# Second MLP weights' block sums made where they are used, on VectorE; q/f/g block sums per pair by accumulating transfers

## The chip, the cores and the metric

The kernel runs on one core of a Trainium2 chip. It is one program on five engines: TensorE (PE in the profile; PEld is its loading of the stationary operand), VectorE (DVE), ScalarE (ACT), GpSimd (POOL) and SyncE (SP), which only issues transfers here. Each engine works through its own list of instructions in order and waits on semaphores. Sixteen DMA engines carry the transfers. PE writes to the eight banks of PSUM, the other data lie in SBUF, inputs and intermediate results in DRAM. The metric is the device time of one execution in microseconds (us), as the median of several.

## The reference

A decoder trunk on x of 1024 tokens by 1024 features, float32, two layers. Each layer is a token mixer and a squared-ReLU MLP, each followed by a residual sum and a layer norm.

```python
def hgrn2_mixer(h, w_in, lb, norm_g, w_out):       # layer 0
    q, fz, v, g = jnp.split(h @ w_in, 4, axis=-1)  # w_in: (1024, 4096)
    q = silu(q); f = lb + (1 - lb) * sigmoid(fz); k = 1 - f
    # 8 heads of 128; S_t = diag(f_t) S_{t-1} + k_t v_t^T, o_t = S_t^T q_t
    o = recurrence(q, k, v, f)
    o = rms_norm(o) * norm_g                       # per head
    return (o * silu(g)) @ w_out

def conformer_conv_mixer(h, ...):                  # layer 1
    a, gate = split(h @ w_pw1 + b_pw1)
    u = depthwise_conv(a * sigmoid(gate), width 31, causal) + b_dw
    return silu(layer_norm(u)) @ w_pw2 + b_pw2

for i in range(2):
    x = layer_norm(alpha * x + mixer(x))
    x = layer_norm(alpha * x + square(relu(x @ w1[i])) @ w2[i])   # w1: (1024, 4096), w2: (4096, 1024)
```

## The kernel before

Every product is made in three matmuls: each float32 operand is cut into a rounded high part and the rest (ScalarE casts, VectorE subtracts: `cut`, `split`), and high x high, high x low and low x high are added in PSUM.

The large products of layer 0 and both second MLP products also use a two by two block scheme with seven products instead of eight. Four blocks of each operand are combined into seven forms, numbered and taken in `ORDER = (1, 2, 6, 5, 7, 3, 4)`. With weight blocks w0 to w3, the forms are w0 (1), w1 (2), w0 + w2 + w3 (6), w2 + w3 (5), w0 + w2 (7), the sum of all four (3) and w3 (4). Where and by whom these sums are made is what this case is about.

The stages, in order of time:

- **Value product** (to about 100 us). x and the value weights are loaded; `add_v` makes the weights' sums, half on POOL (`pool_add`), half on VectorE; `v_products` makes the seven products, `v_out` stores the values to DRAM (`vd`).
- **Pairs and recurrence** (about 100 to 600 us). Twelve pairs in the order `PAIRS`: the q and f columns of a head, or the g columns of two heads. `pair_load` (L534) brings a pair's four blocks in two loads of 512 KB into `r0` and `r1`; `pair_forms` (L542) cuts the forms, with four adds per pair on POOL, and loads the next pair when the last form is cut. `pair_product` (L737) makes one form's 12 matmuls; after every third matmul comes a `slot`, which lets the recurrence take steps at the pace `pace[1]` and counts a tick. `recurrence` (L591) is a generator of steps for one head and half of the tokens: VectorE products, small float32 matmuls, the root mean square (`ss`, with a power on POOL, L472), the result to DRAM (`od`). `swish` and `gate_out` form o * silu(g); for the first seven heads the products of the g gate are on POOL.
- **Output projection and the first MLP product** of layer 0, with norm, whose hidden forms go to DRAM (`hf`).
- **Second MLP product of layer 0** (`down_all`, about 1000 to 1300 us): seven forms times eight column blocks `c`. A column block takes 24 matmuls, one form of the weights (`fw`, tile `dw`, raw tile `dr`, six raw tiles) and one of the hidden values (`fh`, tile `dh`). `Slots.load` loads 512 KB, casts on ScalarE and subtracts on VectorE, four blocks ahead. `spare`, called for five of eight of the made forms in this stage, cuts later weights beside it: one load of 512 KB (`next`) and two stores (`ready`).
- **Convolution mixer** (1300 to 1700 us): 19 of the 31 taps on VectorE, 12 on POOL with the products made on ScalarE. Then the **first and second MLP products of layer 1** (the second from about 1950 us, without `spare`).

The block sums of both layers' w2 are made in DRAM by `block_sums` (L367): 16 calls, one per layer and column block. Each call writes two numbers of a result to the sum's tile (L371, so that the copies start only when that result is there), copies 2 x 1 MB from DRAM to DRAM on SyncE's queue (L372, L373), and adds, later by `gap` ticks each, in three accumulating transfers issued by POOL (L374 of 1 MB, L376 of 512 KB twice). Four calls lie in the value product, ten in the recurrence after a result `o`, two in the convolution stage. `form` then picks what `plan_down` loads.

To about 600 us the orders of PE, POOL and SyncE are those of the program text; VectorE's and ScalarE's orders, and from there on all, are set by a planner at build time.

Of the kernel before, what the change touches and what calls it, by code (L numbers as in the profile page):

```python
# [15 lines left out]
P = 128  # L16
D = 1024
# [18 lines left out]
KBYTES = 220  # L36
NPOOL = 12
# [71 lines left out]
class Forms(Slots):  # L109
# [40 lines left out]
    def ahead(self, n):  # L150

        while self.todo and len(self.queue) < n:
            units = self.todo[0]
            if isinstance(units[0], tuple):
                units = self.todo[0] = [self.unit(*u) for u in units]
            if all([next(u, units) is None for u in units]):
                continue
            self.todo.pop(0)

# [77 lines left out]
def body(ctx, tc, d, out):  # L237
# [127 lines left out]
    sums = {}  # L365

    def block_sums(name, layer, c, after, gap=0):  # L367

        t = sums[name, layer, c] = dram.tile([4, P, 1024], F32, name=f"sum_{name}{layer}{c}")
        v, w = t.rearrange("a p n -> p a n"), d[name][layer, c].rearrange("a p n -> p a n")  # L370
        nc.sync.dma_start(out=t[0:4:2, 0, 0:1], in_=after)  # L371
        nc.sync.dma_start(out=v[:, 0:2], in_=w[:, 0:4:2])  # L372
        nc.sync.dma_start(out=v[:, 2:4], in_=w[:, 0:2])  # L373
        parts = [lambda: nc.gpsimd.dma_start(out=v[:, 0:2], in_=w[:, 2:4], accum_op=ALU.add)]  # L374
        for i in (2, 3):
            parts.append(lambda i=i: nc.gpsimd.dma_start(out=v[:, i], in_=v[:, i - 1], accum_op=ALU.add, max_dma_last_dim=4096))  # L376
        for i, part in enumerate(parts):
            later((i + 1) * gap, part)

    to_sum = [(*of, c) for of in (("w2", 0), ("w2", 1)) for c in range(NFC)]  # L380

    def form(name, layer, c, i):

        w, t = d[name][layer, c], sums[name, layer, c]
        return {1: w[0], 2: w[1], 6: t[2], 5: t[1], 7: t[0], 3: t[3], 4: w[3]}[i]

# [30 lines left out]
    def load_v(raw, m, i0):  # L417
        for j in range(2):
            nc.sync.dma_start(out=raw[:, j], in_=d["wv"][m, i0 + j])
# [44 lines left out]
    nc.sync.dma_start(out=par, in_=d["par"])  # L464
    make_identity(nc, ident)
# [8 lines left out]
    def pool_add(out, x, y):  # L474
        pool.tensor_tensor(out=out, in0=x, in1=y, op=ALU.add)

# [12 lines left out]
    add_v(s7, a0, a2)  # L489
# [9 lines left out]
    outs_v(5)  # L499
    v_products(5)  # L500

    for k in range(4):
        pool.tensor_tensor(out=x01[:, k], in0=x11[:, k], in1=x01[:, k], op=ALU.subtract)
        cut_x(7, x01, (k,))
# [7 lines left out]
    add_v(a1, a0, a1)  # L512
# [16 lines left out]
    r0, r1 = raws((112, 116)).views  # L529
    rs7, vs = view(120, wide_t, F32, "s7"), ring(run(122, 3, 2), rows, "v")  # L530
    fs = ring((152, 156, 128, 132), (2, HT), "fs", F32R)
    PAIRS = [("q", 0), ("q", 1), ("q", 2), ("g", 0), ("q", 3), ("q", 4), ("g", 1), ("q", 5), ("q", 6), ("g", 2), ("q", 7), ("g", 3)]

    def pair_load(p):  # L534
        kind, j = PAIRS[p]
        w = d["wqf" if kind == "q" else "wg"][j]
        nc.sync.dma_start(out=r0, in_=w[0])
        nc.sync.dma_start(out=r1, in_=w[1])

    made = []  # L540

    def pair_forms(p):  # L542
        b0, b1, b2, b3 = r0[:, :HT], r0[:, HT:], r1[:, :HT], r1[:, HT:]

        def put(raw):
            s = fs()
            cut(s[:, 0], s[:, 1], raw)
            made.append(s)

        put(b0)  # L550
        pool_add(rs7, b0, b2)
        pool_add(b2, b2, b3)
        yield
        put(b1)
        pool_add(b0, b2, b0)
        yield
        put(b0)
        pool_add(b1, b0, b1)
        yield
        put(b2)  # L560
        yield
        put(rs7)
        yield
        put(b1)
        yield
        put(b3)
        if p + 1 < len(PAIRS):
            pair_load(p + 1)
        yield

# [20 lines left out]
    def recurrence(h, half):  # L591
# [98 lines left out]
        if 2 * h + half < 10:  # L690
            block_sums(*to_sum.pop(0), o[:2, 0, :1], 24)
# [15 lines left out]
    def swish(out, t, ps=None):  # L707
        sg = p1("sq")
        if ps is None:
            nc.scalar.activation(sg, t, AF.Sigmoid)  # L710
            (vector if out is not t else pool).tensor_tensor(out=out, in0=t, in1=sg, op=ALU.mult)
# [77 lines left out]
    def gate_out(h, half):  # L789
# [3 lines left out]
        def rest():  # L793
            pool.tensor_tensor(out=u, in0=u, in1=g, op=ALU.mult)
# [67 lines left out]
    pair_load(0)  # L862
    forms = pair_forms(0)
    for _ in range(4):
        next(forms)
# [8 lines left out]
            "kt": (rows, 1), "o": (rows, 2), "on": (wide_t, 1), "u": (wide_t, 2), "mask": ((3, P), 1), "rm": ((2, P), 1), "state": ((P,), 2),  # L874
# [3 lines left out]
    rm = p1("rm")  # L878
# [4 lines left out]
    nc.gpsimd.memset(rm, 1.0)  # L883
    load_values(0)

    def all_forms():
        yield from forms
        for p in range(1, len(PAIRS)):
            yield from pair_forms(p)

    ahead_of = all_forms()
    next(ahead_of)
    for p, (kind, j) in enumerate(PAIRS):
        st = {"banks": dict(turn_of)}
        turn_of = {"z": turn_of["a"], "a": turn_of["b"], "b": turn_of["z"]}
        pace[1] = 222 / 308 if p else 0.0
        for i in ORDER:
# [4 lines left out]
            next(ahead_of, None)  # L902
# [248 lines left out]

    def plan_down(layer, fw, fh):
        fw.plan([form("w2", layer, c, i) for i in ORDER for c in range(NFC)])
# [119 lines left out]
    fw = Slots(nc, vector, slots([112, 120, 144, 152, 128, 136, 168], "dw"), raws([192, 196, 200, 204, 160, 164], "dr"), spare, 5, range(12, 56))  # L1273
# [133 lines left out]
    def normalise(half):  # L1407
# [12 lines left out]
        if half == 1:  # L1420
            for of in to_sum:
                block_sums(*of, mv[:2, 0, 4:5])
# [56 lines left out]
    for op, i in steps:  # L1479
# [19 lines left out]
        else:  # L1499
# [3 lines left out]
            if i == NFC - 2:  # L1503
                fw = Slots(nc, vector, slots([64, 72, 144, 152, 200, 208, 112], "dw"), raws([132, 136, 140, 104, 108, 176], "dr"))
# [31 lines left out]
def _layout(inputs):  # L1536
# [14 lines left out]
    r["wqf"] = c(np.stack([cols(w[:, :D], H), cols(w[:, D : 2 * D], H)], 1)).reshape(H, 2, P, 1024)  # L1551
    r["wv"] = c(wide(w[:, 2 * D : 3 * D])).reshape(2, 4, P, 1024)
    r["wg"] = c(cols(w[:, 3 * D :], H)).reshape(H // 2, 2, P, 1024)
# [47 lines left out]
```

## Time and profile before

| | |
|---|---|
| median of 3 runs | 2255.55 us (2252.13 to 2256.26) |
| the profiled execution | 2262.96 us, span 2261.2 us, mean granted clock 0.973 |
| PE busy | 2129.0 us, 94% of the span |
| VectorE, ScalarE, POOL busy | 1471.6, 1034.0, 492.6 us |
| moved by DMA | 508.64 MB, 225 GB/s on average |
| accumulating transfers (software queue) | 33.56 MB |

The page gives each engine's busy time, the span in 40 slices of 56.5 us (busy share in tenths; the granted clock of PE; what the DMA engines moved), the chain of work that ended last, and groups of instructions: line, engine, operation, output<-inputs, shape, count | busy us, mean ns of one | idle time before them and what ended it. A line can be that of a helper: L172 stands for every operation issued through the planner's wrappers. Windows are tables of such numbers for a stretch of time. A busy PE is a PE with a matmul under way; how many matmuls start per microsecond tells more.

### The profile page before, as it was taken

The numbers are of one execution on the slowest core, as the hardware profiler recorded it, in microseconds if no ns is written. First come the engines' busy times: TensorE is split into PE (matmuls) and PEld (weight loads), VectorE is DVE, ScalarE is ACT, GpSimd is POOL, SyncE is SP. The second block draws the span as 40 slices with busy tenths as digits, with TensorE's granted clock in tenths as the row PEclk, the third lists the DMA queues.
The fourth block names the chain that finished last, engine by engine and source line by source line (L and its number), as shares of the span: only waits on it lengthen the run. The fifth ranks groups of instructions, "written<-read, shape, count | busy, mean of one in ns | idle before, by whom it ended". The sixth has DMA issues, their size and how long they took to land.

```text
span 2261.2 us, 27315 instructions
## 1 busy us (share of the span) xinstructions
PE 2129.0 (94%) x10056; PEld 1758.2 (78%) x10056; DVE 1471.6 (65%) x1970; ACT 1034.0 (46%) x1607; POOL 492.6 (22%) x426
## 2 busy tenths in 40 slices
PE   7969878598999999999999999999999999999998
PEld 5747666476788888888888888888887888888887
DVE  8458667476677766665666789789935544555446
ACT  5234243243414655554444477737752543443333
POOL 2231334342110000000000179739700000000001
PEclk8979989798999999999999999999999999999999
DMA  5964868853523777689999875566377798866552
GB/s 201 245 151 131 224 178 207 210 125 103 205 72 124 271 242 278 210 293 380 325 340 339 293 273 193 181 241 235 133 242 252 262 328 309 329 217 191 194 167 103
DMA packets 170952, 508.64 MB, mean 225 GB/s; under 512 B 16192, under 2 KB 45120, under 8 KB 169792
## 3 DMA queue, kind: packets, MB, share of 16 engines
q1 hardware_dynamic: 161856, 473.32, 59.3%
q0 software_dynamic: 8960, 33.56, 8.2%
q8 instruction: 79, 1.29, 0.2%
q14 instruction: 57, 0.47, 0.1%
HBM read 377.32 MB, written 196.61 MB: 254 GB/s over the span
## 4 chain that ended last, share of the span: by engine, by line
PE 75%; DMA 9%; DVE 7%; POOL 4%; issue 2%; ACT 2%; SPq 0%; DVEq 0%; POOLq 0%; ACTq 0%
PE ps L172 75%; POOL cb L172 3%; DMA raw<-in_wqf_dram 2%; DVE qk L172 2%; DMA raw<-in_wg_dram 1%; DMA vd<-vo 1%; DMA u<-od 1%; DMA wa<-ready 1%; DMA raw<-in_w_dram 1%; DVE fs L172 1%; DVE kd L172 1%; DMA vr<-in_wv_dram 1%; DVE at L172 0%; ACT fs L389 0%; POOL raw L172 0%
## 5 line engine op out<-in xcount | busy, mean ns | idle before, releaser
L172 PE MATMUL ps<-dw,dh 128*128 128x512 f32 x2688 | 611.1, 390 | 0.0
L172 PEld LDWEIGHTS ps<-dw,dh 128*128 128x128 f32 x2688 | 504.3, 188 | 104.4 <-ACT dh L69 0.2
L172 PE MATMUL ps<-xf,fs 128*128 128x512 f32 x1008 | 287.7, 425 | 27.5 <-ACT t L752 25.7
L172 PE MATMUL ps<-x1f,fw 128*128 128x512 f32 x1344 | 308.8, 391 | 0.7 <-DVE fw L172 0.3
L172 PEld LDWEIGHTS ps<-x1f,fw 128*128 128x128 f32 x1344 | 251.3, 188 | 53.0 <-DVE fw L172 0.8
L172 PE MATMUL ps<-xa,wa 128*128 128x512 f32 x1152 | 268.8, 392 | 0.0
L172 PEld LDWEIGHTS ps<-xa,wa 128*128 128x128 f32 x1152 | 214.3, 188 | 43.4
L172 POOL TENSOR_TENSOR cb<-cb,prod 128x512 f32<-128x512 f32 x176 | 234.3, 1340 | 17.6 <-ACT prod L1369 7.1
L172 PEld LDWEIGHTS ps<-xf,fs 128*128 128x128 f32 x1008 | 188.6, 200 | 63.3 <-ACT t L752 26.7
L172 DVE TENSOR_TENSOR dh<-dh 128x1024 fp32r<-128x1024 f32 x112 | 136.4, 1223 | 119.5 <-ACT dh L69 116.2
L172 DVE SCALAR_TENSOR_TENSOR ps<-u,par,ps 128x512 f32<-128x512 f32 x288 | 198.7, 750 | 9.8 <-ACT ps L1381 8.4
L172 DVE TENSOR_TENSOR dw<-dr,dw 128x1024 fp32r<-128x1024 f32 x112 | 136.6, 1223 | 101.8 <-ACT dw L69 101.2
L472 POOL TENSOR_TENSOR mv<-mv,nhalf 128x1 f32<-128x1 f32 x32 | 46.3, 1448 | 668.8 <-DVE mv L172 668.8
L69 ACT CAST dh<-dh 128x1024 fp32r<-128x1024 f32 x112 | 117.0, 1051 | 149.7 <-DMA dh<-hf 148.0
L69 ACT CAST dw<-dr 128x1024 fp32r<-128x1024 f32 x112 | 117.4, 1053 | 135.6 <-PE ps L172 124.0
L172 PE MATMUL ps<-xc,wa 128*128 128x512 f32 x768 | 174.4, 389 | 0.0
L172 PEld LDWEIGHTS ps<-xc,wa 128*128 128x128 f32 x768 | 144.1, 188 | 29.8
L1369 ACT ACTIVATE prod<-u,par 128x512 f32<-128x512 f32 x176 | 125.3, 722 | 54.2 <-POOL cb L172 53.5
L1234 POOL COPY next<-ss 128x1 f32<-128x1 f32 x37 | 16.4, 442 | 489.8 <-DVE spare L172 236.1
L172 PE MATMUL ps<-qk 128*128 128x128 f32 (+2 forms) x640 | 60.8, 256 | 59.9 <-DVE qk L172 51.7
L172 PEld LDWEIGHTS ps<-qk 128*128 128x128 f32 (+2 forms) x640 | 54.5, 167 | 78.8 <-issue 39.5
L172 DVE TENSOR_TENSOR wa<-raw,wa 128x1024 fp32r<-128x1024 f32 x55 | 71.3, 1299 | 67.6 <-ACT wa L69 67.5
(193 smaller groups left out, 2908.1 us busy)
## 6 DMA issues: line engine op xcount, KB each, us to landing
wa<-ready SPq DMA_DIRECT2D x122, 512.0 KB, 5.0
dh<-hf SPq DMA_DIRECT2D x112, 512.0 KB, 3.6
ready<-spare SPq DMA_DIRECT2D x74, 512.0 KB, 5.3
sum_w<-in_w_dram SPq DMA_DIRECT2D x32, 1024.0 KB, 7.2
dr<-sum_w SPq DMA_DIRECT2D x64, 512.0 KB, 6.4
raw<-in_w_dram SPq DMA_DIRECT2D x51, 512.0 KB, 4.5
dr<-in_w_dram SPq DMA_DIRECT2D x48, 512.0 KB, 5.3
raw<-in_w1q_dram SPq DMA_DIRECT2D x36, 512.0 KB, 4.2
```

Of the source, the lines that this page charges most:

```text
L69: self.nc.scalar.copy(out=slot[:, 0, c], in_=raw[:, c])
L172: return op(*args, **kw)
L472: nc.gpsimd.tensor_tensor(out=dst, in0=src, in1=nhalf[:, :n], op=ALU.pow)
L1234: nc.gpsimd.tensor_copy(out=raw[:, :1], in_=now)
L1369: nc.scalar.activation(tp, u[:, k : k + HT], AF.Copy, scale=tap(j, k))
```

## The change

It has four parts.

1. `block_sums` and `form` go. A class `Blocks` takes the place of `Slots` for `fw` in both second MLP products. For each form it loads the blocks or pair sums it needs: forms 1 and 2 load two blocks, cut the first, add the second to it on VectorE and store that pair's sum to DRAM; forms 6, 5 and 3 load two and add them on VectorE; 7 and 4 load one.
2. The q, f and g weights lie together (`wp`), and `pair_sums` makes each pair's sums in DRAM, of half the size: two copies of 512 KB on SyncE, accumulating transfers on POOL of 512, 256 and 256 KB. The first three pairs' are issued during the value product, the others three pairs ahead. Each form is loaded by itself (256 KB, five raw tiles, `load_form`, `make_form`). Two sums of value weights (`vsum`) are made in the same way and take the place of two `add_v`.
3. What POOL did elementwise up to 600 us (adds of the value weights, a subtraction on x, the g gate's products) goes to VectorE or falls away with the sums. The convolution's adds stay on POOL.
4. In `recurrence`, the reciprocal is made contiguous (`rt`), the product for `kd` covers half the elements, ScalarE copies the other half, and there is one more step; the pace is 240/308 instead of 222/308.

```diff
+class Blocks(Slots):
...
+    def load(self, pieces=1):
+        (i, c), slot = self.todo.pop(0), self.slots()
+        self.queue.append(slot)
+        w, pair = self.blocks[c]
+        srcs = {1: (w[0], w[2]), 2: (w[1], w[3]), 6: (pair[0], w[3]), 5: (w[2], w[3]), 7: (pair[0],), 3: (pair[0], pair[1]), 4: (w[3],)}[i]
+        got = [self.raws() for _ in srcs]
+        for raw, src in zip(got, srcs):
+            self.nc.sync.dma_start(out=raw, in_=src)
+        if i in (1, 2):
+            self.split(slot, got[0])
+            self.vector.tensor_tensor(out=got[1], in0=got[1], in1=got[0], op=ALU.add)
+            self.nc.sync.dma_start(out=pair[i - 1], in_=got[1])
+        else:
+            if len(got) > 1:
+                self.vector.tensor_tensor(out=got[0], in0=got[0], in1=got[1], op=ALU.add)
+            self.split(slot, got[0])
...
+    def pair_sums(t, w, gap, half=False):
+        n = 1 if half else 2
...
+        nc.sync.dma_start(out=flat(t)[:, 0:2], in_=flat(w)[:, 0 : 4 : n] if n == 2 else flat(w)[:, 0:2])
+        if n == 2:
+            nc.sync.dma_start(out=flat(t)[:, 2:4], in_=flat(w)[:, 0:2])
+        parts = [lambda: nc.gpsimd.dma_start(out=flat(t)[:, 0:2], in_=flat(w)[:, 2:4], accum_op=ALU.add)]
+        for i in (2, 3) if n == 2 else (1,):
+            parts.append(lambda i=i: nc.gpsimd.dma_start(out=flat(t)[:, i], in_=flat(t)[:, i - 1], accum_op=ALU.add, max_dma_last_dim=4096))
...
-            if t == 0 and i in (5, 6, 7, 3):
-                block_sums(*to_sum.pop(0), VO[{5: 5, 6: 6, 7: 5, 3: 6}[i]][0][:2, :1], 24)
+            if t == 3 and i in (2, 5, 6):
+                p = {2: 0, 5: 1, 6: 2}[i]
+                pair_sums(psum[p], d["wp"][p], 8)
...
-        pool_add(out[:, 0], x[:, 0], y[:, 0])
-        vector.tensor_tensor(out=out[:, 1], in0=x[:, 1], in1=y[:, 1], op=ALU.add)
+        for j in range(2):
+            vector.tensor_tensor(out=out[:, j], in0=x[:, j], in1=y[:, j], op=ALU.add)
...
-    add_v(s7, a0, a2)
...
+    sum_v(s7, 0)
+    sum_v(a1, 1)
...
+    def load_form():
...
+        loaded.append(praw())
+        nc.sync.dma_start(out=loaded[-1], in_={1: w[0], 2: w[1], 6: t[2], 5: t[1], 7: t[0], 3: t[3], 4: w[3]}[i])
+
+    def make_form():
+        if loaded:
+            s, raw = fs(), loaded.pop(0)
             cut(s[:, 0], s[:, 1], raw)
             made.append(s)
+            load_form()
...
-        rt = totals[4]
-        vector.reciprocal(cutout(rm, 0, [[P + 1, 2], [2, P // 2]]), cutout(rt, 0, [[1, 2], [2, P // 2]]))
-        kd = p1("kd")
-        mul(kd.rearrange("p a (b n) -> p a b n", n=4), B.rearrange("p a (b n) -> p a b n", n=4), cutout(rm, 0, [[P, 2], [1, P], [0, 4]]))
+        rt, kd = p1("rt"), p1("kd")
+        vector.reciprocal(rt, totals[4])
+        nc.scalar.copy(out=cutout(kd, 4, other), in_=cutout(B, 4, other))
+        mul(cutout(kd, 0, mine), cutout(B, 0, mine), cutout(rt, 0, [[1, 2], [2, P // 2], [0, 4]]))
+        yield
         grow(4)
...
-            pool.tensor_tensor(out=u, in0=u, in1=g, op=ALU.mult)
+            mul(u, u, g)
...
-        pace[1] = 222 / 308 if p else 0.0
+        pace[1] = 240 / 308 if p else 0.0
...
-            next(ahead_of, None)
+            make_form()
+            if i == 6 and p + 3 < len(PAIRS):
+                pair_sums(psum[p + 3], d["wp"][p + 3], 12)
...
-    fw = Slots(nc, vector, slots([112, 120, 144, 152, 128, 136, 168], "dw"), raws([192, 196, 200, 204, 160, 164], "dr"), spare, 5, range(12, 56))
+    fw = Blocks(down_weights(0), nc, vector, slots([112, 120, 144, 152, 128, 136, 168], "dw"), raws([192, 196, 200, 204, 160, 164], "dr"), spare, 5, range(12, 56))
...
-                fw = Slots(nc, vector, slots([64, 72, 144, 152, 200, 208, 112], "dw"), raws([132, 136, 140, 104, 108, 176], "dr"))
+                fw = Blocks(down_weights(1), nc, vector, slots([64, 72, 144, 152, 200, 208, 112], "dw"), raws([132, 136, 140, 104, 108, 176], "dr"))
```

More of the change, by code (lines that the diff above doesn't have):

```diff
@@ L363, in tick, with flat @@
                 job()
[L365 to L376, printed above, removed]
-        for i, part in enumerate(parts):
[L378 to L385, printed above, removed]
+    def pair_sums(t, w, gap, half=False):
+        n = 1 if half else 2
+        def flat(x):
+            return x.rearrange("a p n -> p a n")
+        nc.sync.dma_start(out=flat(t)[:, 0:2], in_=flat(w)[:, 0 : 4 : n] if n == 2 else flat(w)[:, 0:2])
[4 more added lines that the diff above has]
+            parts.append(lambda i=i: nc.gpsimd.dma_start(out=flat(t)[:, i], in_=flat(t)[:, i - 1], accum_op=ALU.add, max_dma_last_dim=4096))
+        parts.append(lambda: summed.append(t))
+        for i, part in enumerate(parts):
+            later((min(i, len(parts) - 2) + 1) * gap, part)
+    summed = []
     def cut(hi, lo, raw):
@@ L860, in last_head @@
         into(half, H - 1, u)
-    pair_load(0)
-    forms = pair_forms(0)
+    for _ in range(5):
+        load_form()
     for _ in range(4):
-        next(forms)
+        make_form()
     v_products(3)
@@ L882, in body @@
         nc.gpsimd.memset(t, 0.0)
-    nc.gpsimd.memset(rm, 1.0)
     load_values(0)
[L886 to L892, printed above, removed]
+    make_form()
     for p, (kind, j) in enumerate(PAIRS):
@@ L1150, in up_half, with down_weights @@
             store(layer, c, i, None, src)
+    def down_weights(layer):
+        return [(d["w2"][layer, c], [dram.tile([P, 1024], F32, name=f"pair{layer}{c}{k}") for k in range(2)]) for c in range(NFC)]
     def plan_down(layer, fw, fh):
[L1153 removed]
+        fw.plan([(i, c) for i in ORDER for c in range(NFC)])
         fh.plan([hf[layer][c][i] for i in ORDER for c in range(NFC)])
```

81 lines of the change are left out of this document (32 added, 49 removed).

## Prediction

> **What bounds the kernel now.** I read the page's slices first, then the windows by stage, then the waits of TensorE and of SyncE, then the chain. From the page:
>
> ```profile
> span 2261.2 us, 27315 instructions
> PEclk8979989798999999999999999999999999999999
> DMA  5964868853523777689999875566377798866552
> PE 75%; DMA 9%; DVE 7%; POOL 4%; issue 2%; ACT 2%; SPq 0%; DVEq 0%; POOLq 0%; ACTq 0%
> ```
>
> The granted clock is below full only in the first ten slices. DMA is nearly full in slices 19 to 22, where the first layer's second MLP product runs. The windows (length; busy us and count of PE, weight loads, DVE, ACT, POOL; clock, DMA share, GB/s) say the same with numbers:
>
> ```profile
> 0.00:100.00 100.00, 83.73 (x336) 67.14 (x336) 69.27 (x81) 40.45 (x62) 25.78 (x23) 0.93 0.69 218
> 100.00:150.00 50.00, 26.29 (x102) 20.96 (x102) 24.08 (x40) 16.30 (x28) 16.07 (x17) 0.80 0.97 232
> 150.00:600.00 450.00, 370.06 (x2177) 304.76 (x2177) 301.77 (x523) 164.55 (x401) 141.21 (x109) 0.91 0.59 160
> 154.30:188.30 34.00, 33.61 (x225) 27.83 (x224) 27.07 (x52) 15.02 (x34) 4.62 (x4) 1.00 0.32 107
> 450.00:500.00 50.00, 44.62 (x288) 36.64 (x287) 39.72 (x71) 20.17 (x51) 19.83 (x16) 0.97 0.57 137
> 1000.00:1300.00 300.00, 300.00 (x1339) 248.57 (x1338) 189.17 (x212) 136.31 (x142) 18.85 (x32) 1.00 0.93 337
> 1000.00:1020.00 20.00, 20.00 (x90) 16.58 (x89) 10.50 (x11) 6.61 (x8) 1.69 (x4) 1.00 1.02 377
> 1020.00:1060.00 40.00, 40.00 (x178) 33.00 (x177) 23.84 (x26) 19.03 (x19) 1.42 (x2) 1.00 1.03 407
> 1700.00:1800.00 100.00, 96.75 (x437) 79.61 (x436) 53.95 (x67) 34.26 (x47) 8.85 (x6) 0.98 0.71 243
> 1950.00:2250.00 300.00, 300.00 (x1325) 248.50 (x1324) 168.03 (x169) 123.61 (x131) 9.59 (x7) 1.00 0.58 200
> 1960.00:1980.00 20.00, 20.00 (x90) 16.57 (x89) 12.34 (x11) 9.65 (x10) 0.00 (x0) 1.00 1.03 414
> ```
>
> So there are two kinds of stage. From 150 to 600 us (q/f/g pairs beside the recurrence) PE starts 4.84 matmuls per us, but 6.62 in an undisturbed stretch (154.3 to 188.3). Both second MLP products (1000 to 1300, 1950 to 2250) keep PE full: anything that delays them is paid whole. What delays the first stage is in PE's waits (us, times, longest; up to 150 us, then 150 to 600), SyncE's waits and three pieces of the chain:
>
> ```profile
> PE ps L172 <- DVE qk L172: 13.6, 1, 13.6
> PE ps L172 <- ACT t L752: 9.2, 1, 9.2
> ```
> ```profile
> PE ps L172 <- DVE qk L172: 42.4, 16, 6.2
> PE ps L172 <- ACT t L752: 16.4, 2, 10.2
> ```
> ```profile
> SPq L371 <- ACT o L689: 130.1, 10, 27.5
> SPq L795 <- POOL u L172: 108.2, 11, 19.9
> ```
> ```profile
> 227.53 12.13 DMA raw<-in_wqf_dram
> ...
> 317.38 12.63 DMA raw<-in_wg_dram
> ...
> 348.93 14.89 DMA raw<-in_wqf_dram
> ```
>
> A pair's two weight loads have one buffer each. They are issued behind a block sum that waits for a recurrence's output (L371), they run beside its DRAM copies, and they take 12 to 15 us each time on the chain. The pool adds, the cuts on DVE and the recurrence line up behind them; the gated output's store (L795) waits for POOL's product too.
>
> **The change part by part.** Instructions and transfers it touches, as groups and DMA rows (the POOLq rows and those with 5.4 and 7.2 us: median from issue to landing; the L87 row: shortest, median, longest issue in ns; the second fence is of 1000 to 1300 us alone):
>
> ```profile
> L172 POOL TENSOR_TENSOR t<-t,sq 128x512 f32<-128x512 f32 x12 | 18.1, 1510 | 80.4 <-ACT sq L710 80.4
> L172 POOL TENSOR_TENSOR u<-u,t 128x512 f32<-128x512 f32 x12 | 18.0, 1501 | 55.3 <-DMA u<-od 39.3 <-DVE ss L172 16.0
> L172 DVE TENSOR_TENSOR qk<-qk,f 128x512 f32<-128x512 f32 x28 | 19.2, 687 | 0.2
> L172 DVE TENSOR_TENSOR kd<-qk,rm 128x1024 f32<-128x1024 f32 x16 | 24.6, 1540 | 0.3 <-PE ps L172 0.3
> L389 ACT CAST fs<-raw 128x512 fp32r<-128x512 f32 x72 | 43.8, 620 | 149.2 <-PE ps L172 70.5 <-DMA raw<-in_wqf_dram 31.3 <-DMA raw<-in_wg_dram 26.2
> L69 ACT CAST dw<-dr 128x1024 fp32r<-128x1024 f32 x112 | 117.4, 1053 | 135.6 <-PE ps L172 124.0 <-issue 3.9 <-DMA hf<-hr 3.2
> L172 DVE TENSOR_TENSOR dw<-dr,dw 128x1024 fp32r<-128x1024 f32 x112 | 136.6, 1223 | 101.8 <-ACT dw L69 101.2
> sum_w<-in_w_dram POOLq DMA_DIRECT2D x16, 1024.0 KB, 12.4
> sum_w<-sum_w POOLq DMA_DIRECT2D x32, 512.0 KB, 7.2
> L87 SPq DMA_DIRECT2D dr<-sum_w x64: 319/320/1614, 1032.3 to 2141.5; - x64
> ```
> ```profile
> DMA packets 29050, 101.20 MB, mean 337 GB/s; under 512 B 3168, under 2 KB 4192, under 8 KB 29032
> ready<-spare SPq DMA_DIRECT2D x48, 512.0 KB, 5.4
> dr<-in_w_dram SPq DMA_DIRECT2D x15, 512.0 KB, 7.2
> ```
>
> Pairs, 150 to 600 us: ten block sums leave (2 MB of copies and 2 MB of accumulating transfers each), with the SyncE wait of 130.1 us. Twelve half-size sums come, three pairs ahead, and every form has its own 256 KB load, five buffers deep and some ten forms before use: 84 loads for 24. At the best 50 us (450 to 500: 288, or 5.76 per us) 2177 matmuls take 378 us, 72 less. Bounds: only the waits behind `t` go (-16), or all runs at 6.62 (329 us, -121). I take -72, because that window still holds waits but few of them.
>
> Its cover: DVE takes 24 products from POOL (24 x 0.69 = 17 us); the half-length kd product saves 16 x (1.54 - 0.69) = 14; the reciprocal keeps its size. DVE's 302 us become 305 of 378, 81%, and the undisturbed stretch has 80% with PE full. ACT gets 16 copies of 0.62 us (10 us) on 165 of 450, SyncE 60 more issues of 0.32 us (19 of 378): nothing. The recurrence has 18 steps for 17 and a pace 240/222 as fast: nothing. Without DVE's cover this is the second rival. POOL's power op now stands behind accumulating transfers that wait for one another (12.4 and 7.2 us at twice the size); issues lie 12 of a pair's 28 slots apart (of 378 / 12 = 31 us: 13 us). On SyncE a sum's load waits for its transfer, and the recurrence's stores and value loads queue behind it; the forms' lead of some ten covers the loads, the stores have none. Bounds for both 0 and +12 (one landing of 12.4), I take +4, nearer the end where the issues are 13 us apart.
>
> Start, 100 to 150 us: the two waits of 22.8 us hang on the first pair loads, queued behind stores and sums. Now the loads go ahead but four of seven forms come from transfer sums. Bounds -5 and -25; I take -18.
>
> Value product, to 100 us: two sums move from engines to transfers (the s7 form needs one after a 12.4 us landing), other adds from POOL to DVE, which has 69 of 100 us busy and loses a competitor. Bounds -3 and +10; I take +2, nearer the end where a load comes in time.
>
> The last two block sums (near 1660 us) leave: PE misses 3.3 us from 1700 to 1800; I take -3, bounds 0 and -5.
>
> First layer's second product, from 1000 us: per column block, seven loads of 0.524 MB become twelve and two stores: 40 loads and 16 stores more, 29.4 MB. 101.2 + 29.4 = 130.6 MB. The rate decides, since DMA is at 93% already. At 407 (loads alone) they take 321 us, +21; at 337 (as now, stores a third) 388 us, +87. I take 377, the slice with both: 346 us, +46, less 6 for the blocks fetched ahead of 1000 us: +40. DVE gets 40 adds of 1.22 us: 189 + 49 = 238 of 300, beside.
>
> Here a rule speaks against the change: the Trainium skill, DMA: Bandwidth & Descriptors, Where 436 GB/s comes from, says that for transfers between HBM and SBUF a core's HBM share of about 358 GB/s binds, not the fabric. The 407 and 414 GB/s rows contradict it for loads. By the rule this term would be 365 - 300 - 6 = 59, estimated from the page, and the time 2236.
>
> Second layer: the same 29.4 MB on 200 GB/s. Only the first two forms are tight: 16 blocks of 4 transfers, 2.1 MB in 5.4 us of PE (24 x 300/1339). At 377 that is 5.6 us, +3. Also six raw tiles serve three blocks in flight, and a tile is free again only after landing 7.2, cast 1.05, two DVE ops 2.4 and the store 5.4: 16.1 us, or 5.4 per block, with nothing to spare. Bounds 0 and 16 x 2.1 = 34 (landing and store 10 us); I take +8.
>
> Sum: -72 + 4 - 18 + 2 - 3 + 40 + 8 = -39. The profiled execution took 2262.96 us (span 2261.2), which gives 2224; the median of the runs shown is 7.4 lower, so 2217.
>
> **The rivals.**
> 1. The tile ring: SyncE is one queue, so a pair's store that waits for its add holds up the next loads, and at a full DMA landing and store take 10 us: 23.5 us per three blocks, 7.8 per block. 32 blocks x 2.4 = 77; the first layer's other three two-load forms at 337 GB/s (2.6 MB with the spare traffic, 7.6 us) add 24 x 2.2 = 53. 130 instead of 48: 2299, slower. It decides from 87 us on. For it: 93% DMA and a loop without slack; against: 407 GB/s is there when asked for.
> 2. DVE becomes the bound of the pairs: 42.4 us of PE waits are on the recurrence's qk. At 5.2 matmuls per us the stage takes 419 (-31) and the start gives 8: 2268, slower. Against it: the stretch at 6.62 with DVE at 80%.
> 3. The transfers fit: 407 GB/s (+15) and nothing in the second layer: 2184.
> 4. Mixed loads and stores can't go above today's 337 GB/s: +81 instead of +40: 2258, no change. For it: the 377 slice is 20 us short; against: no engine waited at 337, so it was a demand.
>
> The page's 2236 lies between rival 4 and the forecast, inside the forecast's own range.
>
> That it doesn't do what it says touches only the convolution, whose adds stay on POOL; nothing is priced there.
>
> **How the numbers follow.** Forecast 0.40 (own range 2195 to 2240), rival 1 0.18, rival 2 0.12, rival 3 0.20, rival 4 0.10. Forecast and 3 are faster, 0.60, and 0.04 of 4; slower are 1 and 2, 0.30; same (within 0.2%, 4.5 us, which is what a measurement here can tell) 0.06 of 4. The range 2175 to 2278 holds all but rival 1 and the tails.
>
> **What would show it.** Right: PE starts on out-projection some 85 us earlier, the waits on pair loads are gone, and the window after it at full clock; the first layer's second product takes about 340 us with DMA near 1.0 and PE waiting for ACT or DVE on dw. Wrong: PE still full there (rival 3), DMA well under 1.0 while PE waits and SyncE waits on a pair's add (rival 1), or DVE above 90% from 100 to 500 us (rival 2).

## The result, and the profile after

The changed kernel takes 2246.9 us (median of six runs, 2244.3 to 2249.6) against 2254.5 (six runs, 2251.9 to 2256.7). The ratio is 0.9967 with a 95% interval of 0.9954 to 0.998: 0.3% faster, 8 us where 39 were forecast. The profiled execution took 2245.4 us. From its page (the span, the granted clock, DMA's busy share and the chain):

```profile
span 2243.3 us, 27717 instructions
PEclk9999999999999999999999989999999999999999
DMA  9866655434358687899997955375455898999762
PE 44%; DMA 5%; POOL 3%; DVE 3%; ACT 2%; issue 1%; SPq 0%; DVEq 0%; POOLq 0%; ACTq 0%
```

No slice of the first ten falls under nine tenths of the clock any more (from 100 to 150 us it is still 0.86, for 0.80 before), and a new drop stands in slice 24 (1290 to 1346 us), in the convolution. PE's 44% of the chain can't be set against the 75% before: this chain could be followed back to 912 us only, so that its shares add up to 58% of the span, where those of the kernel before add up to 99%. The stages, from the timeline (each lasts from its first matmul to the first of the next; us; the first column is when the output projection starts, the last ones the span of the profiled execution and the median of all runs). The rows below the first two are the experiments. Each was run beside the kernel before, whose median was 2254.5 to 2260.3 us in these sessions; the ratios given further down go by the runs beside:

| kernel | pairs end | output projection and 1st product, layer 0 | 2nd product, layer 0 | convolution, and first half of layer 1's 1st product | its second half | 2nd product, layer 1 | span | median |
|---|---|---|---|---|---|---|---|---|
| before | 586.6 | 411.7 | 308.4 | 467.6 | 174.2 | 312.6 | 2261.2 | 2254.5 |
| changed | 491.1 | 411.4 | 350.5 | 495.1 | 174.1 | 321.1 | 2243.3 | 2246.9 |
| early copies | 496.4 | 410.2 | 330.6 | 462.3 | 174.1 | 320.9 | 2194.5 | 2194.9 |
| before, early copies | 585.4 | 411.0 | 312.2 | 466.8 | 174.2 | 312.2 | 2261.8 | 2262.6 |
| before, late copies | 584.2 | 411.6 | 336.4 | 508.7 | 174.2 | 312.6 | 2327.7 | 2327.5 |
| one store | 491.6 | 410.6 | 351.0 | 490.4 | 174.1 | 312.7 | 2230.4 | 2233.1 |
| no store | 492.0 | 410.6 | 367.7 | 464.1 | 174.1 | 335.0 | 2243.5 | 2245.5 |
| ten raw tiles | 488.1 | 410.5 | 353.3 | 494.9 | 174.1 | 316.5 | 2237.5 | 2240.9 |
| block sums alone | 507.7 | 411.1 | 354.3 | 494.9 | 174.1 | 320.5 | 2262.5 | 2260.7 |
| the rest alone | 619.6 | 410.6 | 308.5 | 467.2 | 174.2 | 312.7 | 2292.8 | 2294.6 |
| early copies, one store | 493.2 | 410.7 | 321.1 | 464.0 | 174.1 | 312.6 | 2175.7 | 2179.6 |
| and gates on VectorE | 491.9 | 410.8 | 319.8 | 463.1 | 174.1 | 312.7 | 2172.4 | 2174.5 |
| and copies still earlier | 492.2 | 417.6 | 336.8 | 462.6 | 174.1 | 313.3 | 2196.6 | 2198.0 |
| before again | 584.9 | 411.4 | 308.3 | 469.3 | 174.2 | 312.6 | 2260.7 | 2258.9 |

So the first stage gave 95.5 us, and three later stages took back 42.1, 27.5 and 8.4. The windows of the changed kernel that answer to those before (length; busy us and count of PE, weight loads, DVE, ACT, POOL; clock, DMA share, GB/s):

```profile
0.00:100.00 100.00, 87.55 (x360) 70.74 (x360) 58.59 (x86) 42.01 (x64) 11.86 (x19) 0.97 0.95 278
100.00:150.00 50.00, 35.32 (x177) 29.16 (x178) 28.91 (x57) 20.53 (x34) 6.59 (x8) 0.86 0.68 169
150.00:490.00 340.00, 318.51 (x2013) 265.12 (x2012) 252.89 (x511) 162.05 (x398) 40.72 (x38) 0.98 0.53 148
902.50:1253.00 350.50, 319.63 (x1377) 260.37 (x1375) 231.09 (x251) 136.73 (x143) 31.90 (x40) 0.96 0.92 353
1253.00:1748.00 495.00, 471.27 (x2145) 386.99 (x2145) 376.95 (x529) 284.86 (x446) 257.27 (x202) 0.97 0.56 200
1922.00:2243.00 321.00, 307.58 (x1346) 253.52 (x1344) 212.58 (x213) 124.01 (x133) 10.46 (x8) 0.98 0.74 270
```

From 150 to 490 us PE starts 5.92 matmuls per us (4.84 from 150 to 600 before). Both second products and the convolution have lost their full PE. The convolution stage before, as a window:

```profile
1306.70:1774.40 467.70, 463.94 (x2146) 383.81 (x2144) 362.63 (x520) 275.46 (x434) 260.92 (x203) 1.00 0.62 216
```

Not all of the loss is idle time. PE is busy for 471 us in place of 464 with the same matmuls, at a clock of 0.97 in place of 1.00, so 7 of the convolution's 27.5 us are slower matmuls. In the first layer's second product it is 320 us in place of 308 at 0.96, 11 of the 42.1. PE's waits in the first of these products, and then in the convolution stage (1250 to 1750 us; in the same stage before, only 3.2 us for `wa<-ready` and 0.3 for `cb`; the wait for `xa` ends at 1251.3 us, ahead of the stage's first matmul as the table counts it):

```profile
PE ps L201 <- ACT dw L70: 15.1, 4, 8.8
PE ps L201 <- ACT dh L70: 10.2, 1, 10.2
```
```profile
PE ps L201 <- DMA wa<-ready: 9.5, 1, 9.5
PE ps L201 <- ACT y L1436: 4.7, 1, 4.7
PE ps L201 <- ACT z L1450: 4.5, 2, 4.3
PE ps L201 <- DVE xa L201: 4.4, 1, 4.4
```

The chain tells what the first wait of the second fence hangs on (start, us, what):

```profile
1247.09 1.05 ACT spare L1236
...
1278.68 0.95 ACT spare L1236
...
1294.86 1.23 DVE spare L201
1296.11 5.39 DMA ready<-spare
1301.55 3.54 DMA wa<-ready
1305.14 1.22 PE ps L201 x2
```

These are the background copies that `spare` makes beside the second product: one load of a later weight, a cast, a subtraction and two stores, 1.57 MB, with one buffer. In the kernel before, the last of them was stored 9 us ahead of the convolution's first matmul (1306.7 us):

```profile
1297.62 0.36 SPq L1231 DMA_DIRECT2D ready<-spare  x1
```

In the changed kernel the last two stores are issued 41 to 43 us after it (1253.0 us):

```profile
1294.15 2.27 SPq L1240 DMA_DIRECT2D ready<-spare  x2
```

The planner, which sets the order of every engine's list here, has spread the last copies among the convolution's own loads, casts and subtractions.

### The profile page after: what moved, and what is told of

Its sections match the earlier page's. It is cut to its first block, busy times and chain, and to the rows that moved or that the text cites. A ratio compares the mean times of both kernels' runs of the same rounds, so it can differ in the third digit from the quotient of the medians.

```text
span 2243.3 us, 27717 instructions
## 1 busy us (share of the span) xinstructions
PE 2124.4 (95%) x10056; PEld 1749.5 (78%) x10056; DVE 1527.5 (68%) x2078; ACT 1044.3 (47%) x1623; POOL 378.0 (17%) x337
## 4 chain that ended last, share of the span: by engine, by line
PE 44%; DMA 5%; POOL 3%; DVE 3%; ACT 2%; issue 1%; SPq 0%; DVEq 0%; POOLq 0%; ACTq 0%
PE ps L201 44%; POOL cb L201 3%; DMA next<-in_w_dram 1%; DMA next<-in_wpw_dram 1%; DMA hf<-ht 1%; DMA dr<-in_w_dram 1%; DMA pair<-dr 1%; DVE ps L201 1%; DMA dh<-hf 0%; DVE spare L201 0%; ACT spare L1236 0%; DVE dr L201 0%; ACT prod L1378 0%; ACT dw L70 0%; DMA raw<-in_w_dram 0%
## 5 line engine op out<-in xcount | busy, mean ns | idle before, releaser
L201 PE MATMUL ps<-dw,dh 128*128 128x512 f32 x2688 | 622.8, 394 | 32.2 <-ACT dw L70 20.3
L201 PEld LDWEIGHTS ps<-dw,dh 128*128 128x128 f32 x2688 | 509.9, 190 | 144.2 <-ACT dw L70 22.4
L201 PE MATMUL ps<-xf,fs 128*128 128x512 f32 x1008 | 274.5, 410 | 11.7 <-ACT t L764 11.7
L201 PE MATMUL ps<-xa,wa 128*128 128x512 f32 x1152 | 273.5, 396 | 10.3 <-DMA wa<-ready 9.5
L201 PEld LDWEIGHTS ps<-xf,fs 128*128 128x128 f32 x1008 | 180.6, 192 | 44.4 <-ACT t L764 12.1
L201 DVE SCALAR_TENSOR_TENSOR ps<-u,par,ps 128x512 f32<-128x512 f32 x288 | 204.5, 751 | 13.4 <-ACT ps L1390 9.9
L201 PE MATMUL ps<-xc,wa 128*128 128x512 f32 x768 | 174.2, 389 | 0.0
L201 DVE TENSOR_TENSOR dr<-dr 128x1024 f32<-128x1024 f32 x80 | 97.3, 1221 | 40.7 <-DMA dr<-pair 19.8
L70 ACT CAST wa<-raw 128x1024 fp32r<-128x1024 f32 x55 | 57.8, 1050 | 127.8 <-PE ps L201 103.8
```

The costliest lines, as they stand in the source:

```text
L70: self.nc.scalar.copy(out=slot[:, 0, c], in_=raw[:, c])
L201: return op(*args, **kw)
```

## The experiments

**Theory A (spill)** says that the convolution's 27.5 us come from copies that still run in it. **Rival B** says that the convolution's own work stands worse, whatever the copies do. **Rival C**, for a remedy, says that the first product has no room for them.

**Copies earlier, in the changed kernel.**

```diff
-    fw = Forms(..., spare, 3, range(44))
+    fw = Forms(..., spare, 5, range(44))
-    fw = Blocks(down_weights(0), ..., spare, 5, range(12, 56))
+    fw = Blocks(down_weights(0), ..., spare, 3, range(10, 56))
```

> The changed kernel, with the background copies of the convolution's weights (one load, cast, subtract and two stores each) begun at a higher rate in the first layer's first product (5 of 8 forms for 3 of 8) and at a lower one in its second product (3 of 8 for 5 of 8). Theory A (spill): the 27 us that the convolution stage took longer come from these copies still running when it begins; now they end before it, and the stage takes 470 us (495 with the change as it was, 468 before). Some ten copies of 1.57 MB leave the second product too, 16 MB or 42 us at 377 GB/s, so it goes from 350 to 310-325 us, and the whole to 2180-2200 us. Rival B (the convolution's own work on VectorE, ScalarE and GpSimd stands worse with the new order, whatever the copies do): the convolution stage stays at 490 or more, the second product alone shortens, 2205-2215 us. Rival C (the first product has no room): its 411 us grow by what the second product saves, 2240 us or more.

Measured: 2194.9 us, ratio to before 0.9711 (0.9687 to 0.9736). The convolution stage takes 462.3 us with a full PE and full clock, the first product 410.2 as before, the second 330.6, a little more than expected:

```profile
1237.00:1699.50 462.50, 461.99 (x2146) 382.88 (x2145) 365.36 (x522) 275.99 (x437) 253.94 (x197) 1.00 0.57 203
```

Three numbers in two lines turned a gain of 8 us into one of 64 (2.9%, against 2258.7 us of the kernel before beside it). Rivals B and C fall at this dose.

**The same edit in the kernel before** (control; there `Blocks` is `Slots`).

```diff
-    fw = Forms(..., spare, 3, range(44))
+    fw = Forms(..., spare, 5, range(44))
-    fw = Slots(..., spare, 5, range(12, 56))
+    fw = Slots(..., spare, 3, range(10, 56))
```

> Control: the kernel before with the same two rates. Theory A: its second product already keeps TensorE full, and its copies ended 9 us before the convolution began, so nothing is to be had: 2249-2257 us, second product 308 us, convolution stage 465-468. Rival B: the same. If the first product has no room (rival C), it grows here too and the time goes above 2262.

Measured: 2262.6 us, ratio 1.0014 (0.9998 to 1.0031): nothing. The time is above the 2262 us named as rival C's sign, but the kernel before took 2258.7 us beside it and the first product didn't grow (411.0); the second took 312.2 us, 4 more. Where the copies end in time and PE is full, moving them is worth nothing. It is the change that made their place matter.

**The cause put into the kernel before.** Copies at 1 of 8 forms and then 7 of 8 (instead of 3 and 5), nothing else.

```diff
-    fw = Forms(..., spare, 3, range(44))
+    fw = Forms(..., spare, 1, range(44))
-    fw = Slots(..., spare, 5, range(12, 56))
+    fw = Slots(..., spare, 7, range(12, 56))
```

> The kernel before with the suspected cause put into it and nothing else: the background copies at 1 of 8 forms in the first product and 7 of 8 in the second, so that they come to stand behind the convolution's first weight loads in SyncE's queue, as in the changed kernel. Theory A (spill): the convolution stage goes from 467 to 480-500 us though every other part of the kernel is as before; the second product, with 17 copies' 27 MB more, goes from 308 to 308-330; total 2270-2310 us. If the longer convolution stage comes from another part of the change (rival B): 467 stays, and only the second product may grow.

Measured: 2327.5 us, ratio 1.0296 (1.0276 to 1.0317). The convolution stage takes 508.7 us, 41 more, and the second product 336.4; both are above what was expected. PE's waits in the convolution stage (1332 to 1841 us) are of the same kinds as in the changed kernel:

```profile
PE ps L172 <- DMA wa<-ready: 21.1, 3, 17.5
PE ps L172 <- ACT y L1430: 4.6, 1, 4.6
PE ps L172 <- ACT z L1444: 4.5, 2, 4.3
```

Taken out, put in and left alone: theory A is shown. The other kernels agree. In the nine of the table's fourteen profiles where the last store of a copy is issued before the convolution's first matmul or within 3 us of it, the stage takes 462.3 to 469.3 us; in the five where it comes 35 to 53 us after, 490.4 to 508.7. How much of the 27.5 us is the late weight load and how much the copies' place on ScalarE and VectorE, no run separates, since the planner orders all of it anew each time; PE's waits give 9.5 us to the load.

**One stored pair sum instead of two.**

```diff
-2: (w[1], w[3]), ... 3: (pair[0], pair[1])
+2: (w[1],), ...      3: (pair[0], w[1], w[3])
...
-        if i in (1, 2):
+        if i == 1:
...
```

> The changed kernel with one pair sum per column block stored instead of two: w1+w3 isn't made ahead, and the form of all four blocks loads w1 and w3 beside the stored w0+w2. 12 loads and 1 store for 12 and 2: 4.2 MB less in each layer. Bandwidth theory (the second products are bound by bytes): first layer's 350 us less 11 at 377 GB/s, 339; second layer's 321 less 0 to 4. Copies' spill (theory A): the copies end in the convolution as now, so that its stage keeps 485-495. Together 2231-2238 us. If the stores' place in SyncE's queue holds the loads up (ring theory, as in the first rival of the prediction), each product gains more than its bytes: 325 or less and 313, 2215 us.

Measured: 2233.1 us, ratio 0.9889 (0.987 to 0.9907). The second layer's product is back at 312.7 us, with no wait of PE left. The first layer's stays at 351.0 though 4.2 MB are gone. The total lies where the bandwidth theory put it (2231 to 2238), but by luck: it had 339 us for the first of these products and 317 to 321 for the second. Where the first one's time is lost has moved. One 20 us window of the changed kernel (end of form 2), and two of this one (end of form 2, and form 3, which loads three blocks now):

```profile
1002.50:1022.50 20.00, 11.18 (x36) 8.58 (x36) 12.67 (x13) 6.18 (x6) 0.18 (x1) 0.72 1.03 415
```
```profile
1002.20:1022.20 20.00, 20.00 (x90) 16.58 (x89) 17.17 (x19) 9.78 (x11) 2.29 (x2) 1.00 1.02 401
1162.20:1182.20 20.00, 15.24 (x56) 11.43 (x55) 15.19 (x15) 8.04 (x8) 1.30 (x2) 0.88 1.03 414
```

**No stored pair sum: 14 loads, the same bytes.**

```diff
+        srcs = {1: (w[0],), 2: (w[1],), 6: (w[0], w[2], w[3]), 5: (w[2], w[3]), 7: (w[0], w[2]), 3: (w[0], w[2], w[1], w[3]), 4: (w[3],)}[i]
...
```

> The changed kernel without any stored pair sum: every form adds up its blocks from the weights themselves (1, 1, 3, 2, 2, 4 and 1 loads: 14 loads for 12 loads and 2 stores, the same 7.3 MB per column block, and 7 adds for 5). Bandwidth theory, any byte the same: first layer's second product 350 +-4, second layer's 321 +-3. Store theory (stores cost more than loads, or hold loads up in SyncE's queue): 320-335 and 313. Theory A: the copies come to stand earlier in SyncE's queue here, nearly all ahead of the convolution, so the convolution stage takes 468-475. Theory A with bandwidth: 2222-2228 us; rival B with bandwidth: 2245-2250; theory A with stores: 2195-2212.

Measured: 2245.5 us, ratio 0.994 (0.992 to 0.996). Both products are slower, 367.7 and 335.0, so that neither the bandwidth theory (same bytes, same time) nor the store theory holds. Of the 36.3 us that the first of them waits for `dw`, 29.4 stand in the form that loads four blocks: 2.1 MB of weights and 0.5 MB of hidden values per block of 5.4 us, which is 490 GB/s even without the background copies, where the windows above moved 415. What bounds these products is how the transfers are spread over the forms, more than their sum. All but two of the copies' stores came to stand ahead of the convolution here, the last 2 us behind its first matmul, and its stage took 464.1: theory A once more.

**Ten raw tiles for six in the second layer's product.**

```diff
-  fw = Blocks(down_weights(1), ..., raws([132, 136, 140, 104, 108, 176], "dr"))
+  fw = Blocks(down_weights(1), ..., raws([132, 136, 140, 104, 108, 176, 184, 188, 192, 196], "dr"))
```

> The changed kernel with ten raw tiles in place of six for the second layer's second product. The prediction put this stage's 8 us down to the ring: six tiles, two per block in the first two forms, free again only after landing, cast, add and store. If the ring is the cause, the wait of 5.2 us for dw goes and the stage takes 312-314 us (321 with six tiles): 2238-2240 us in all. If the transfers of those sixteen blocks are what is late (three of 0.5 MB and one of 1 MB per block in 5.4 us, which is 485 GB/s), more tiles change nothing: 319-322, 2245-2249.

Measured: 316.5 us, half way between the two expectations (2240.9 us in all, 0.9918 with 0.989 to 0.9947; the first stage was 3 us quicker too). The wait of 5.2 us for `dw` is gone, as it should be if the ring is its cause, so the ring is 4.6 of that stage's 8.4 us. What the other 3.8 hang on isn't shown; PE still waits 1.3 us for `dh` and 1.5 for two subtractions. The 485 GB/s of the expectation counts the hidden values twice: their load is 512 KB (and not 1 MB, as the expectation for the copies still earlier, below, has it too), and the four transfers of a block in 5.4 us are 390 GB/s.

**The block sums' move alone** (part 1 on the kernel before), and **the rest alone** (parts 2 to 4, with `block_sums` left as it was). The first on the kernel before, the second on the changed one:

```diff
...
-            if t == 0 and i in (5, 6, 7, 3):
-                block_sums(*to_sum.pop(0), ...)
...
-        if 2 * h + half < 10:
-            block_sums(*to_sum.pop(0), o[:2, 0, :1], 24)
...
-    fw = Slots(...)
+    fw = Blocks(down_weights(0), ...)
...
```
```diff
...
+        if 2 * h + half < 10:
+            block_sums(*to_sum.pop(0), o[:2, 0, :1], 24)
...
-    fw = Blocks(down_weights(0), ...)
+    fw = Slots(...)
...
```

> The kernel before with the first part of the change alone: the second MLP weights' block sums made in their own stages on VectorE, ten block sums gone from the first stage and two from the convolution; the q/f/g sums stay on GpSimd with the pair's two single-buffered loads. The prediction took the whole of the first stage's gain as one term. If the sums' transfers and the 130 us of SyncE waits were the larger cause: out-projection starts 50-70 us earlier than before (586.6). If the single-buffered pair loads and GpSimd's adds were: 10-30. The stages behind: first layer's second product +35 to +45, convolution 0 to +27 by where the copies come to stand, second layer's +8. Total 2230-2255 us in the first case, 2265-2310 in the second.

> The changed kernel without its first part: the block sums stay in the first stage as transfers, the q/f/g sums go to accumulating transfers too, and the elementwise work leaves GpSimd. First stage: the rest of the 95 us that the whole change won there, 25-45 if the two parts add (550 us instead of 586.6), more transfers than before and every sum's load behind two kinds of waits on SyncE; if transfers are what bounds that stage, nothing or a loss. The stages behind as before: 308, 468 and 312 us. Total 2212-2235 us, or 2250-2275 in the second case.

Measured: 2260.7 us, ratio 1.0 (0.9981 to 1.002), and 2294.6, ratio 1.015 (1.011 to 1.019). Part 1 alone ends the pairs 78.9 us earlier, more than either case expected, and brings all three later costs (45.9, 27.3, 7.9). The other parts alone end them 33.0 us later, a larger loss than expected; together they are worth 95.5. The two don't add: the rest is worth 16.6 us after part 1, and costs 33 without it. The windows from 150 to 490 us, part 1 alone and then the rest alone, show why:

```profile
150.00:490.00 340.00, 307.23 (x1886) 254.71 (x1885) 263.86 (x469) 146.09 (x362) 103.11 (x72) 0.95 0.22 73
```
```profile
150.00:490.00 340.00, 251.71 (x1489) 209.19 (x1490) 198.34 (x400) 122.42 (x289) 63.55 (x64) 0.85 0.94 251
```

DMA is at 0.22 without the block sums, 0.53 in the changed kernel, and 0.94 where the pair sums come on top of the block sums. There PE waits 47.3 us for the forms (`fs`) from 100 to 620 us. With part 1 alone the pair loads, in the same single buffers, land much sooner. Their rows of these 340 us, in the kernel before and with part 1 alone (the last number is the median from issue to landing, in us):

```profile
raw<-in_wqf_dram SPq DMA_DIRECT2D x10, 512.0 KB, 9.7
raw<-in_wg_dram SPq DMA_DIRECT2D x6, 512.0 KB, 13.7
```
```profile
raw<-in_wqf_dram SPq DMA_DIRECT2D x10, 512.0 KB, 4.1
raw<-in_wg_dram SPq DMA_DIRECT2D x8, 512.0 KB, 3.7
```

**Both remedies, then two more steps.** Early copies and one stored sum; to that, the one-column copies that gate the residual's loads made on VectorE instead of GpSimd; to that, copies at 7 of 8 forms and then 2 of 8 from the 8th to the 44th. The two further steps:

```diff
-                nc.gpsimd.tensor_copy(out=y[half][:, t, :1], in_=after)
+                nc.vector.tensor_copy(out=y[half][:, t, :1], in_=after)
```
```diff
-    fw = Forms(..., spare, 5, range(44))
+    fw = Forms(..., spare, 7, range(44))
-    fw = Blocks(down_weights(0), ..., spare, 3, range(10, 56))
+    fw = Blocks(down_weights(0), ..., spare, 2, range(8, 44))
```

> Both earlier edits in one: the copies early (5 of 8, then 3 of 8), and one stored pair sum per column block. If the two causes are separate, their gains add: the convolution stage 462-466 us as with the early copies alone, the second layer's second product 312-313 as with the one store alone. The first layer's: 330.6 us with the early copies, of which about half the waits (TensorE started 66 and 53 matmuls in 40 us for 178) stand at the end of the form of the second blocks, whose second load and store now go: 318-325. Together 2178-2186 us. If the first layer's product is bound by how much it moves in all, it loses only 4.2 MB, 11 us, or nothing where the form of all four blocks (three loads now) takes it back: 2186-2190.

> The same with the eight one-column copies that hold back the residual's loads (y before the first layer's second product) made on VectorE in place of GpSimd. In the changed kernel GpSimd took 11.1 us over them while VectorE ran without a gap, SyncE stood for 10.3 us in front of the first residual load and DMA was at 0.1 of its share; TensorE then waited 10.2 us for a block of the activations. If this queueing is its cause: the wait at the start of the product goes and 5 to 10 us with it, 2170-2180 us. If the residual's bytes (4.2 MB with the stores of the first product's last blocks) are its cause: no change against the kernel without this edit (within 3 us).

> The early copies, the one stored pair sum and the VectorE gates (2174 us), with the copies moved further ahead: 7 of 8 forms in the first product, then 2 of 8 forms and none among the last 12. The first layer's second product took 319.8 us against 308 before, so 12 us are left there at most; some ten copies leave it, 16 MB. If the bytes beside the product are what is left: 310-314 us, 2165-2169 in all. If its first two forms are (three transfers and a 1 MB activation load per block in 5.4 us): 318-320, no change. Rival C again (no room in the first product, whose DMA stands at 0.9 in its second half with 5 of 8): its 411 us grow by 5 or more and the total is above 2174.

Measured: 2179.6 us (0.9644, 0.9619 to 0.9668), 2174.5 (0.9627, 0.9605 to 0.9649) and 2198.0 (0.9727, 0.9709 to 0.9745). The gains of the first two add as expected. The gates are worth 5 us of the medians with intervals that overlap, and 1.3 us of the product, so their share isn't settled. Nor can they show anything about the queue: the kernel they were put into has no such queue any more, though its gates are on GpSimd. The first 20 us of the product, in the changed kernel (DMA share 0.56), in the one with early copies and one store (1.00) and in the one with the gates (0.98):

```profile
902.50:922.50 20.00, 20.00 (x90) 16.57 (x89) 9.42 (x11) 4.84 (x7) 10.29 (x8) 1.00 0.56 194
```
```profile
903.80:923.80 20.00, 20.00 (x89) 16.54 (x89) 13.20 (x15) 6.84 (x10) 6.95 (x8) 1.00 1.00 364
```
```profile
902.70:922.70 20.00, 20.00 (x90) 16.58 (x89) 12.70 (x22) 6.46 (x10) 0.00 (x0) 1.00 0.98 339
```

The last step goes too far: the first product takes 417.6 us, with 3.6 us of waits for its own weights, and the second one gets slower again (336.8), with a 16.8 us wait for `dw` some 33 us after its start. Rival C is true at that dose. The best of these kernels is the one with all but the last step, 3.7% faster than before.

**The kernel before once more.**

> The kernel before as it is, for a second profile. Its first profiled execution was 8 us above its median, the changed kernel's 1.5 below its own, and the prediction took 7.4 us off for that. If the excess lay in the first stage (where the transfers' times vary), out-projection starts at 576-583 us here in an execution of 2252-2257 us, and the stages behind it keep 411, 308, 468 and 312; if it lay behind it, out-projection starts at 585-588 again.

Measured: a profiled execution of 2262.6 us again, with the stages of the first within 2 us; the runs beside it have a median of 2258.9. The expectation needed one of 2252 to 2257 us, so where the spread of this kernel lies stays open.

## Why the prediction came out as it did

By stages, profile against profile, 2224 was forecast and 2245.4 measured. The 21 us: 11.5 more gained in the first stage, 30.5 more lost in the convolution, 2.5 in the two second products. Another 9 us lie in the base: 7.4 were taken off because the profiled execution of before stood above its median, and the changed kernel's stands 1.5 below its own. The second profile of the kernel before stands only 3.7 above the median of its runs, so the 7.4 may in part have been chance.

- **The step that failed: the convolution stage, priced at -3, measured +27.5.** The prediction counted what left that stage (two block sums) and not what could come into it. It named the copies only as bytes in the product ahead. A copy goes through DMA, ScalarE, VectorE and DMA again with one buffer, and five of eight blocks of 5.4 us ask for one every 8.6 us. In the kernel before, the last was stored 9 us ahead of the convolution; in the changed one the last six stores came to stand behind its first matmul, and 27.5 of the 95.5 us went there. Whether the full DMA or the order that the planner made for the longer list of loads put them there, no run separates. With no stored sum, at the same bytes, all but two stores are in time, but that product is 17 us longer too.
- **Pairs -72 and +4, start -18, value product +2: -84, measured -95.5.** By 150 us PE had started 537 matmuls for 438, 99 more, or 17 us at 5.76 per us (16 forecast); 78 us came after (68 forecast), at a rate of 5.92 where 5.76 was taken. VectorE has 74% of that stretch for the 81% forecast. The size held, the cause only in part: the late pair loads were put down to their single buffers as well, but part 1 alone keeps these and gains 78.9, with the loads landing in 4.1 and 3.7 us for 9.7 and 13.7. They were late because of the transfers beside them, and the pair sums by transfers are paid in the same way.
- **The first layer's second product +40, measured +42.1.** The size was right by luck, its working was not. In place of 130.6 MB at 377 GB/s, 123.8 MB went at 353 in the mean, 415 in some windows and under 300 in others. The 42.1 us are 31 of waits (15.1 and 1.0 for `dw`, 10.2 for `dh`, 4.4 for `xa`) and 11 of slower matmuls, for which the prediction had no term. Before the wait for `dh` SyncE stood 10.3 us at the residual's loads and DMA idled, and the chain leads from there to PE; in four kernels where SyncE didn't stand so (early copies, with one store, with the gates, no store) this wait is 5.2, 3.3, 5.3 and 0.4 us, so the queue is some 5 to 10 us of the loss. Bytes alone don't set this time, as the runs with 4.2 MB less (351.0) and with the same bytes spread otherwise (367.7) show.
- **The second layer's +8, measured +8.4**, about half of it by the ring that was named. As time, 5.8 us of it are waits for `dw` and the rest slower matmuls (PE busy for 307.6 us in place of 304.9, at a clock of 0.98).
- **The rivals.** The tile ring exists, at 4.6 us in the second layer's product. In the first layer's no run took it out, and the loss of both products is 50.5 us together, where this rival had 130. VectorE didn't become the bound. The transfers didn't fit, and the mixed rate was no fixed 337 either: windows with loads and stores ran at 415. By the Trainium skill, DMA: Bandwidth & Descriptors, Where 436 GB/s comes from, about 358 GB/s should have bound them; the trace disagrees here (415) as it did before (407).
- **What would show it** was right for the projection's start, for the waits on pair loads and for `dw`. No row was named for the stage behind the crowded one.

## What to carry to other kernels

When a stage is given more transfers, follow everything else that shares its queues to where it ends: background work that was just in time spills into the next stage, and a rate of 3 or 5 in 8 decided over some 50 us here. Count a wait with the slower matmuls around it: in the 20 us window with the longest wait for `dw` the granted clock was 0.72, and 36 matmuls took 11.18 us where 90 take 20.00. Cost transfers form by form and not by their sum, since a burst isn't paid by a quiet stretch later. And test two parts of a change that use one resource together as well as alone: one that cost 33 us alone was worth 17 behind the other.

## What was not expected of the hardware

One copy of a single column on GpSimd took 10.3 us, with 0.18 as the median of its kind (shortest, median, longest ns):

```profile
L1289 POOL COPY y<-dw x8: 181/182/10272, 901.7 to 912.6; 128x1 f32<-128x1 f32 x8
```
```profile
SPq L1290 <- POOL y L1289: 10.8, 2, 10.3
```

While it lasted, to 911.9 us, VectorE ran two-operand float32 instructions of 0.7 to 1.2 us without a gap. That alone doesn't explain it: with early copies and one stored sum VectorE has no gap beside the eight copies either (904.8 to 911.8 us), and each takes 0.66 to 1.20 us:

```profile
L1289 POOL COPY y<-dw x8: 663/868/1198, 904.8 to 911.6; 128x1 f32<-128x1 f32 x8
```

By the Trainium skill (SBUF — State Buffer, SBUF: two separate sides) VectorE, with two inputs in SBUF, and GpSimd, reading SBUF, lock a shared port pair against each other for a whole instruction. The copies of 0.66 to 1.20 us agree with that; one of 10.3 us, over some ten instructions, isn't explained by it. What made it so long stays open.

A DMA share near one says little of the bytes: with accumulating and DRAM to DRAM transfers among them 0.94 of the engines' time went for 251 GB/s (the rest alone, above), where loads and stores of SBUF fill 1.03 at 415.
